# Low parts of the weights fetched in attention: made by GpSimd instead of VectorE

## The chip, the cores and the metric

The kernel runs on one core of a Trainium2 chip. Its metric is the device time of one execution in microseconds (us); lower is better. TensorE is called PE here, VectorE DVE, ScalarE ACT, GpSimd POOL and SyncE SP, as the profile's rows have them. SP only issues DMAs here.

## The reference, cut to what matters

One layer of a decoder, 1024 rows by 1024 columns, in float32:

```
h = rms_norm(x, attn_norm_w)
q, k, v, u, g = split(h @ w_in)            # 1024 x 7168 weights
# branch A: 8 heads, each with two score maps of 64 columns
p = softmax(q1 k1^T * scale + bias) - lam * softmax(q2 k2^T * scale + bias)
a = rms_norm(p @ v, subln_w) * (1 - lam_init);  y_a = a @ w_proj_attn
# branch B: causal convolution over 31 rows, for each channel
c = conv(u_a * sigmoid(u_b)) + conv_b
y_b = silu(layer_norm(c)) @ w_proj_conv
x = x + (sigmoid(g_a) * y_a + sigmoid(g_b) * y_b) @ w_out
h = rms_norm(x, ffn_norm_w)
x = x + (silu(h @ w_gate) * (h @ w_up)) @ w_down
```

## The kernel before, in words

**Products in three parts.** Each large product of float32 numbers is made of three fast ones. A number is split in a high part, rounded to a shorter format by ACT (`split_hi`, a copy, L120), and a low part, the rest (`value - high`, a subtraction). The product is high x high + high x low + low x high (`mm3`, L168 to L170). So every block of weights that is loaded (`wraw`, 128 x 1024 numbers, two buffers) needs a high part (`whi`) and a low part (`wlo`, three buffers each). `wsplit` makes both: first the high part on ACT, then the low part through `low`. The function `low` asks a switch, `low_by_pool`: if it is set, the subtraction is POOL's (L131), else DVE's (L125, inside `split_lo`, which serves all other splits, too).

**Order of the work.** The stages are: the opening and the first stage (0 to about 300 us in the profile: the products for u, some of v and the first head's q and k, with the first half of the convolution on DVE beside them), attention (about 300 to 815), the two projections with the layer norm of the convolution, the merge, and the channel mixer. The switch is set at the end of the opening and cleared after the first stage, so attention's low parts are DVE's.

**Attention** is a list of 64 steps: 8 heads (h) with 8 blocks of 128 rows (i). A step of block i has these parts. PE makes scores (`sc`, L1289 and L1290) from the parts of q (`qs`) and k (`ks`). DVE adds the bias (`tb`, one buffer, loaded by SP from `t_d` for each head) and finds the minimum (L1291: writes `E` and `mn`). ACT takes the exponential (L1296). DVE joins the two maps of a head (L1303, L1304, L1306: both inputs of L1306 are in SBUF). One step later PE turns `E` in blocks (`pT`, L1328), ACT makes the high part of the turned block (`ph`), DVE the low part (`pl`, from the turned block in PSUM). For each pair of blocks PE multiplies with v (`pW`), ACT copies the result (`ar`), PE turns it back (`pB`), and at a head's end comes the norm (`pS`, L1362). Of the two tiles `ph` and `pl` POOL sets a corner to zero for each pair (L1318, L1319); both have one buffer, so POOL waits there until PE has used the pair before.

Beside these 64 steps PE works through a list of products from h (`pg`, L168 to L170, where the weights come in): the next head's q and k, and g. The function `more` puts them between the steps. They need new weights: `ws` loads them (SP, into `wraw`) and splits them two blocks ahead of use (`ws.ahead = 2`). The products for q and k are scaled on DVE (L807), turned (`pQ`) and split again (L822, L824, `klo`), and shifted between halves of the partitions by DMAs (L826 to L837).

In the background DVE runs the second half of the convolution: channel tiles 4 to 7, 30 taps each (`bg`, L594, `acc` = `acc` + weight x `u`). The sums of tiles 0 to 3 (first stage) are in PSUM, those of tiles 4 to 7 in SBUF. A tile's sums are stored by SP (`c_d`), and POOL issues a DMA that adds them up over the tiles (L578, `cs_d`). POOL also issues the DMAs that make `t_d` (L776).

At the end of attention the finished heads are read back (`early`), split (`aTh`, `aTl`), and the first projection begins (`pg<-aTh,whi`).

**Who sets the order.** Each engine works through its own queue strictly in turn, and an instruction that waits holds all behind it. The queues are filled by a scheduler in the building step, which follows the program and its own idea of how long things take; so a change of one instruction's engine can move many others. The steps' shares of background taps are set by numbers in the kernel (`slack_of`), which don't change.

Of the kernel before, what the change touches and what calls it, by code (L numbers as in the profile page):

```python
# [57 lines left out]
def kernel(  # L58
# [68 lines left out]
    low_by_pool = [False]  # L127
# [1117 lines left out]
        due -= int(due)  # L1245
    while late:
        late.pop(0)[1]()
    low_by_pool[0] = False
    pcv_ctx.close()
    pgs.pop()  # L1250
    pg2_ctx.close()
# [264 lines left out]
    with after(m):  # L1516
        for _ in fill:
            pass
    inatt[0] = False
    del pms[1:]  # L1520
    at_ctx.close()

# [612 lines left out]
```

## Time and profile before

| what | us |
|---|---|
| median of 3 runs (1726.63 to 1727.03) | 1726.91 |
| span of the profiled execution | 1725.7 |
| median less that span: what lies around it | 1.2 |
| DVE busy in the span | 1275.4 |
| ACT busy in the span | 862.5 |
| DVE busy from 0 to 300 us | 228.14 |
| POOL busy from 0 to 300 us | 199.05 |

How to read it: a row of the profile names the source line (L125), the engine, the operation, the tiles as out<-in with buffer numbers left out, the shape, and the count; then busy us, mean ns of one, and the idle time of the engine just before with what ended it. A row of the timeline starts with the start and the length in us, and ends in brackets with the idle time before it, where there was any; `x3` means three merged. A row of the waits names who waited for whom, the sum in us, the number of times and the longest. PE's matmuls overlap, so their lengths are longer than the time from one start to the next.

### The profile page before, as it was taken

The numbers are of one execution on the slowest core, as the hardware profiler recorded it, in microseconds if no ns is written. First come the engines' busy times: TensorE is split into PE (matmuls) and PEld (weight loads), VectorE is DVE, ScalarE is ACT, GpSimd is POOL, SyncE is SP. The second block draws the span as 40 slices with busy tenths as digits, with TensorE's granted clock in tenths as the row PEclk, the third lists the DMA queues.
The fourth block names the chain that finished last, engine by engine and source line by source line (L and its number), as shares of the span: only waits on it lengthen the run. The fifth ranks groups of instructions, "written<-read, shape, count | busy, mean of one in ns | idle before, by whom it ended". The sixth has DMA issues, their size and how long they took to land.

```text
span 1725.7 us, 25863 instructions
## 1 busy us (share of the span) xinstructions
PE 1714.6 (99%) x9243; PEld 1477.9 (86%) x9243; DVE 1275.4 (74%) x2128; ACT 862.5 (50%) x1958; POOL 219.1 (13%) x207
## 2 busy tenths in 40 slices
PE   9999999999999999999999999999999999999999
PEld 7997889998998998988788888888888888888887
DVE  7675889898988888878687769966676666575544
ACT  5333335767777776756556325633333333333332
POOL 3997851000000000000000000000000000000000
PEclk9999999999999999999999999999999999999999
DMA  6344445336345344343973683245455445598663
GB/s 208 116 126 132 131 151 154 104 109 171 104 127 147 115 125 138 101 136 130 333 238 118 200 296 119 74 135 164 147 170 170 154 141 164 175 355 285 217 215 130
DMA packets 261604, 281.64 MB, mean 163 GB/s; under 512 B 16546, under 2 KB 181986, under 8 KB 261475
## 3 DMA queue, kind: packets, MB, share of 16 engines
q1 hardware_dynamic: 254160, 267.71, 48.3%
q0 software_dynamic: 5680, 9.39, 2.6%
q10 hardware_dynamic: 1634, 2.89, 0.5%
q8 instruction: 73, 1.20, 0.3%
q14 instruction: 57, 0.46, 0.1%
HBM read 181.84 MB, written 85.50 MB: 155 GB/s over the span
## 4 chain that ended last, share of the span: by engine, by line
PE 92%; DMA 3%; DVE 2%; ACT 1%; issue 1%; POOL 0%; SPq 0%; DVEq 0%; POOLq 0%; ACTq 0%
PE acc L980 29%; PE acc L488 12%; PE pg L168 12%; PE pg L169 12%; PE pg L170 12%; PE wo L1850 3%; PE sc L1290 2%; PE sc L1289 2%; PE pT L1328 2%; PE pg L1106 1%; DVE acc L594 1%; PE pW L168 1%; PE pW L169 1%; PE pW L170 1%; PE pQ L815 1%
## 5 line engine op out<-in xcount | busy, mean ns | idle before, releaser
L594 DVE SCALAR_TENSOR_TENSOR acc<-u,cw,acc 128x1023 f32<-128x1023 f32 (+14 forms) x240 | 303.4, 1264 | 23.2 <-ACT acc L588 20.7
L170 PE MATMUL pg<-whi,hT_lo 128*128 128x256 f32 x704 | 200.2, 285 | 0.0
L168 PE MATMUL pg<-whi,hT_hi 128*128 128x256 f32 x704 | 199.7, 285 | 0.4 <-DVE v L125 0.4
L169 PE MATMUL pg<-wlo,hT_hi 128*128 128x256 f32 x704 | 199.5, 284 | 0.0
L125 DVE TENSOR_TENSOR wlo<-draw,whi 128x1024 fp32r<-128x1024 f32 x75 | 91.7, 1223 | 83.4 <-ACT whi L120 78.9
L120 ACT CAST whi<-draw 128x1024 fp32r<-128x1024 f32 x75 | 79.1, 1055 | 129.5 <-PE acc L488 114.3
L169 PEld LDWEIGHTS pg<-wlo,hT_hi 128*128 128x128 f32 x704 | 134.4, 191 | 1.8
L170 PEld LDWEIGHTS pg<-whi,hT_lo 128*128 128x128 f32 x704 | 134.3, 191 | 1.8
L168 PEld LDWEIGHTS pg<-whi,hT_hi 128*128 128x128 f32 x704 | 134.0, 191 | 2.1 <-DVE v L125 0.6
L120 ACT CAST whi<-wraw 128x1024 fp32r<-128x1024 f32 x90 | 94.7, 1052 | 70.6 <-PE pg L169 32.6
L488 PE MATMUL acc<-wlo,whi 128*128 128x512 f32 x308 | 119.8, 389 | 0.0
L488 PE MATMUL acc<-whi,wlo 128*128 128x512 f32 x308 | 119.8, 389 | 0.0
L1296 ACT ACTIVATE E<-E,mn 128x640 f32<-128x640 f32 (+7 forms) x128 | 99.8, 781 | 30.8 <-DVE mn L1291 29.2
L168 PE MATMUL pg<-hT_hi,whi 128*128 128x512 f32 x288 | 114.4, 397 | 0.1
L169 PE MATMUL pg<-hT_lo,whi 128*128 128x512 f32 x288 | 113.7, 395 | 0.0
L170 PE MATMUL pg<-hT_hi,wlo 128*128 128x512 f32 x288 | 113.7, 395 | 0.0
L120 ACT CAST whi<-s 128x1024 fp32r<-128x1024 f32 x54 | 56.9, 1053 | 104.9 <-PE acc L980 101.8
L125 DVE TENSOR_TENSOR wlo<-wraw,whi 128x1024 fp32r<-128x1024 f32 x75 | 93.3, 1246 | 12.6 <-ACT whi L120 12.3
L1291 DVE CUSTOM_DVE_ANT_0 E<-sc,tb 128x512 f32<-128x512 f32 (+3 forms) x128 | 74.2, 585 | 33.2 <-PE pT L1328 16.1
L980 PE MATMUL acc<-h_hi,whi 128*128 128x512 f32 x240 | 93.4, 389 | 0.0
L980 PE MATMUL acc<-h_lo,whi 128*128 128x512 f32 x240 | 93.4, 389 | 0.0
L980 PE MATMUL acc<-h_hi,wlo 128*128 128x512 f32 x240 | 90.1, 389 | 0.0
(370 smaller groups left out, 4589.7 us busy)
## 6 DMA issues: line engine op xcount, KB each, us to landing
wraw<-in_w_gate_up_dram SPq DMA_DIRECT2D x44, 512.0 KB, 4.7
wraw<-in_w_in_dram SPq DMA_DIRECT2D x38, 512.0 KB, 4.0
qs<-qs SPq DMA_DIRECT2D x96, 128.0 KB, 2.3
wd<-in_w_down_dram SPq DMA_DIRECT2D x44, 256.0 KB, 3.1
tdT<-wd SPq DMA_DIRECT2D x88, 128.0 KB, 4.8
draw<-sdS SPq DMA_DIRECT2D x44, 256.0 KB, 3.7
draw<-tdT SPq DMA_DIRECT2D x44, 256.0 KB, 3.7
wraw<-in_w_in_dram SPq DMA_DIRECT2D x32, 256.0 KB, 3.3
```

Source lines behind the costliest of these rows:

```text
L120: act.copy(dst, src)
L125: last_lo[0] = dve.tensor_tensor(dst, src, f32(hi), op=ALU.subtract).ins
L168: pe.matmul(o, lh, rh, start=start, stop=False)
L169: pe.matmul(o, lh, rl, start=False, stop=False)
L170: last_mm[0] = pe.matmul(o, ll, rh, start=False, stop=stop).ins
L488: m = pe.matmul(o[s_][i][:], l_[:, ts], r_[:, 512:], start=start and j + y_ == 0, stop=j == n - 1 and y_ == 2, skip_group_check=not start,)
L594: dve.scalar_tensor_tensor(a_, us[c][:, : S - n], cw[:, c, t : t + 1], a_, op0=ALU.mult, op1=ALU.add)
L980: last_mm[0] = pe.matmul(o[:], a_[x_][:, k, :], b_[y_][:, k, :], start=start and k + x_ + y_ == 0, stop=k == 3 and x_ == 1, skip_group_che ...
L1289: pe.matmul(o[:, :w], qh[:, qs], k, start=True, stop=False)
L1291: dve.tensor_tensor_reduce(e[:, ks], o[:, :w], tb[:, S - nk + c0 : S - nk + c0 + w], 1.0, mn[:, j : j + 1] if c0 else 3.0e38, ALU.add, ALU ...
L1296: act.activation(e[:, :nk], e[:, :nk], AF.Exp, bias=mn[:, j : j + 1], scale=-1.0, accum_out=l[:, j : j + 1])
L1850: last_mm[0] = pe.matmul(o[s_][i][:], A[u_], B[v_], start=start and j + y_ == 0, stop=j == 3 and y_ == 2, skip_group_check=not start,).ins
```

## The change

The line that clears the switch moves from the end of the first stage to the end of attention:

```
--- before
+++ after
     while late:
         late.pop(0)[1]()
-    low_by_pool[0] = False
     pcv_ctx.close()
...
         for _ in fill:
             pass
     inatt[0] = False
+    low_by_pool[0] = False
     del pms[1:]
     at_ctx.close()
```

So the low parts of all weights that are fetched in attention, those for q, k and g and the first ones of the projection, are POOL's: 30 instructions of 128 x 1024. Their data, sizes and buffers stay. Lines after 1248 have numbers smaller by one in the changed kernel, up to the line that came in. The scheduler writes the queues anew from the start of attention; from the first projection on they are the same again.

Here is POOL's queue at the end of head 2 and the start of head 3, before. `pl` and `ph` are the memsets, the numbers are buffers.

```order
L1319 MEMSET pl_628_5090 128x128
L1318 MEMSET ph_627_5089 128x128
L1319 MEMSET pl_669_5359 128x128
L1318 MEMSET ph_668_5358 128x128
L1319 MEMSET pl_705_5547 128x128
L1318 MEMSET ph_704_5546 128x128
```

The same place of POOL's queue in the changed kernel:

```order
L1318 MEMSET pl_628_5090 128x128
L1317 MEMSET ph_627_5089 128x128
L1318 MEMSET pl_669_5359 128x128
L1317 MEMSET ph_668_5358 128x128
L131 TENSOR_TENSOR wlo_602_4877<-wraw_600_4873,whi_601_4876 128x1024
L131 TENSOR_TENSOR wlo_701_5515<-wraw_699_5511,whi_700_5514 128x1024
L131 TENSOR_TENSOR wlo_742_5686<-wraw_740_5683,whi_741_5685 128x1024
L1318 MEMSET pl_705_5547 128x128
```

Three low parts now stand between memsets of one pair and of the next; the first of them comes behind the memsets of buffers 669 and 668.

The end of attention in POOL's queue, before; `cs_d` is the DMA that adds the last channel tile's sums.

```order
L1319 MEMSET pl_1423_9593 128x128
L1318 MEMSET ph_1422_9592 128x128
L1319 MEMSET pl_1450_9707 128x128
L1318 MEMSET ph_1449_9706 128x128
L578 DMA cs_d_145<-c_d7_144 512x256
```

The same place in the changed kernel:

```order
L1318 MEMSET pl_1423_9593 128x128
L1317 MEMSET ph_1422_9592 128x128
L578 DMA cs_d_145<-c_d7_144 512x256
L131 TENSOR_TENSOR wlo_1457_9772<-wraw_1455_9769,whi_1456_9771 128x1024
L1318 MEMSET pl_1450_9707 128x128
L1317 MEMSET ph_1449_9706 128x128
```

The DMA and a low part now come ahead of the last pair's memsets.

PE's queue at this place, before, where the last pair of blocks of the last head is turned and multiplied:

```order
L1328 MATMUL pT_1451_9710<-ident_78,E_1427_9608 128x128
L1328 MATMUL pT_1454_9742<-ident_78,E_1444_9690 128x128 x2
L1348 MATMUL pB_1460_9803<-ident_78,ar_1441_9686 128x128 x2
L168 MATMUL pW_1462_9811<-ph_1449_9706,vh7_9162 128x256
L169 MATMUL pW_1462_9811<-pl_1450_9707,vh7_9162 128x256
```

The last rows of the same in the changed kernel:

```order
L168 MATMUL pg_1458_9775<-hT_hi_324,whi_1402_9469 128x512
L169 MATMUL pg_1458_9775<-hT_lo_325,whi_1402_9469 128x512
L170 MATMUL pg_1458_9775<-hT_hi_324,wlo_1403_9470 128x512
L1347 MATMUL pB_1460_9803<-ident_78,ar_1441_9686 128x128 x2
L168 MATMUL pW_1462_9811<-ph_1449_9706,vh7_9162 128x256
L169 MATMUL pW_1462_9811<-pl_1450_9707,vh7_9162 128x256
```

Between the pT of buffer 1454 and the pB there are now 19 matmuls of `pg` (the last three are shown), most of which stood further up before.

More of the change, by code (lines that the diff above doesn't have):

```diff
@@ L1247 @@
         late.pop(0)[1]()
-    low_by_pool[0] = False
     pcv_ctx.close()
@@ L1519 @@
     inatt[0] = False
+    low_by_pool[0] = False
     del pms[1:]
```

## The prediction

> **What bounds the kernel now.** I read the page first, then the waits and the busy time of the stretch that the change touches, the instruction groups of VectorE and GpSimd (DVE and POOL in the rows), and at last the timeline at single places.
>
> ```profile
> span 1725.7 us, 25863 instructions
> PE 1714.6 (99%) x9243; PEld 1477.9 (86%) x9243; DVE 1275.4 (74%) x2128; ACT 862.5 (50%) x1958; POOL 219.1 (13%) x207
> PE 92%; DMA 3%; DVE 2%; ACT 1%; issue 1%; POOL 0%; SPq 0%; DVEq 0%; POOLq 0%; ACTq 0%
> 300.00:815.00 515.00, 512.77 (x3435) 469.51 (x3434) 441.36 (x977) 363.14 (x1200) 18.11 (x71) 1.00 0.44 124
> PE sc L1289 <- DMA ks<-klo: 1.1, 1, 1.1
> PE sc L1290 <- DMA qs<-qs: 0.8, 1, 0.8
> PE pg L168 <- ACT sgg L639: 0.4, 1, 0.4
> PE pg L169 <- DVE aTl L125: 0.2, 1, 0.2
> ```
>
> The first three lines are the page: TensorE (PE) is busy 99% of the span and is 92% of the chain that ended last. The fourth is attention, from 300 to 815 us; its figures are PE, weight loads, DVE, ACT and POOL busy, then the granted clock (1.00) and the DMA share. PE stands idle for 515 - 512.77 = 2.23 us there, DVE for 515 - 441.36 = 73.64, and POOL is nearly free. The last four are all that PE waited for between 300 and 830 us: 2.5 us, and no row names a low part of a weight. So DVE's time is not what sets the end. The median of the runs, 1726.91, is the span and 1.2 us around it; I take my terms from the span and add them to 1726.91.
>
> **What is moved.** The order shows 30 low parts going from DVE to POOL, and nothing else leaves or comes; the other rows are the same work in another order. The groups between 300 and 815 us give the price on DVE, and the group of the stage before gives it on POOL, for the same shape.
>
> ```profile
> L125 DVE TENSOR_TENSOR wlo<-wraw,whi 128x1024 fp32r<-128x1024 f32 x30 | 36.6, 1219 | 2.8 <-ACT whi L120 2.7
> L131 POOL TENSOR_TENSOR wlo<-wraw,whi 128x1024 fp32r<-128x1024 f32 x15 | 36.2, 2414 | 49.6 <-ACT whi L120 49.6
> L594 DVE SCALAR_TENSOR_TENSOR acc<-u,cw,acc 128x995 f32<-128x995 f32 (+14 forms) x122 | 153.7, 1260 | 2.9 <-ACT acc L588 2.8
> L1306 DVE SCALAR_TENSOR_TENSOR E<-E,rl,E 128x640 f32<-128x640 f32 (+3 forms) x64 | 52.1, 814 | 0.6
> L807 DVE TENSOR_TENSOR qkraw<-qkraw,r 128x1024 f32<-128x1024 f32 x14 | 17.0, 1218 | 0.0
> ```
>
> DVE loses 30 x 1.219 = 36.6 us of work, POOL gains 30 x 2.414 = 72.4 us. POOL has 515 - 18.11 = 497 us free, so its own time hides.
>
> **Is a low part late?** It is needed when TensorE first loads it. The shortest lead that POOL's work of before, put in the new order, leaves inside attention is at the start of head 3. By buffer number this is the high part cast at 461.76, and its low part's first matmul is at 479.14.
>
> ```profile
> 461.76 1.07 ACT L120 CAST whi<-wraw 128x1024 fp32r<-128x1024 f32 x1
> 463.41 1.22 DVE L125 TENSOR_TENSOR wlo<-wraw,whi 128x1024 fp32r<-128x1024 f32 x1
> 468.65 0.21 POOL L1319 MEMSET pl<- 128x128 f32 x1 [21.20 <-PE pW L169]
> 468.81 0.21 POOL L1318 MEMSET ph<- 128x128 f32 x1
> 479.14 0.28 PE L169 MATMUL pg<-wlo,hT_hi 128*128 128x256 f32 x1
> ```
>
> On DVE it was done at 464.63, 14.5 us early. In the new order POOL reaches it only behind two memsets that wait for a pW matmul; they end at 469.0, so the low part ends at 469.0 + 2.4 = 471.4, still 7.7 us early. Behind it on POOL stands the next low part (done by 473.9) and nothing that others wait for sooner. The raw buffer it reads comes free 6.9 us later than before, and the SP queue holds the next raw load until then, with the ks copies of head 3 behind it.
>
> ```profile
> 468.26 0.72 SPq L836 DMA_DIRECT2D ks<-klo  x1
> 498.41 0.22 PE L1289 MATMUL sc<-ks,qs 128*128 128x128 f32 x1
> ```
>
> Those copies were issued at 468.26 and are first read at 498.41, so 30 us cover a delay of a few. Cost of lateness: 0, and if the cover went, PE would wait by the missing part.
>
> **What DVE and POOL do to each other.** In attention they have hardly been busy together, but before it there are places where they were.
>
> ```profile
> 49.02 4.78 DVE L272 TENSOR_TENSOR lprod<-lamt 128x64 f32<-128x64 f32 x2
> 56.94 2.57 DVE L125 TENSOR_TENSOR wlo<-wraw,whi 128x1024 fp32r<-128x1024 f32 x1
> 48.95 7.12 POOL L896 TENSOR_TENSOR F<-hT_hi,hT_lo 128x1024 f32<-128x1024 f32 x3
> 56.04 9.09 POOL L905 TENSOR_TENSOR F<-F,F 128x1024 f32<-128x1024 f32 x3
> 67.46 2.40 POOL L905 TENSOR_TENSOR F<-F,F 128x1024 f32<-128x1024 f32 x1
> 11.38 0.69 DVE L125 TENSOR_TENSOR hT_lo<-px,hT_hi 128x512 fp32r<-128x512 f32 x1 [0.74 <-ACT hT_hi L120]
> 10.95 2.38 POOL L1133 TENSOR_TENSOR vwl<-wraw,vwh 128x1024 fp32r<-128x1024 f32 x1 [9.63 <-ACT vwh L120]
> ```
>
> Two DVE products of 64 columns took 4.78 us, 2.39 each, just what one POOL instruction beside them took (7.12 / 3 = 2.37). A DVE low part took 2.57 instead of 1.22, and POOL's three took 9.09 where one alone takes 2.40. These DVE operations read two tensors from SBUF. The one at 11.38 reads one of its two from PSUM and kept its 0.69 beside a running POOL instruction. So one waits for the other's whole instruction if both of DVE's inputs lie in SBUF. [...]
>
> In attention the convolution taps (L594) have their sums in SBUF for the four channel tiles left, and L1306 and L807 read two SBUF tensors as well: 153.7 + 52.1 + 17.0 = 222.8 us of DVE's time. So a DVE operation will often meet a low part on POOL. One low part costs DVE between 0 (none meets it) and 2.41 us (one meets it at its start). I take the middle, 1.2, since a DVE operation of this kind is running or next about half the time (222.8 of 515). That is 30 x 1.2 = 36 us of waiting in place of 36.6 us of work: **DVE gains nothing**, 0.6 us. At the upper end it has 72.3 - 36.6 = 35.7 us more, still under its 73.64 us of idle time.
>
> **The end of attention.** PE has small gaps here that the list of waits leaves out.
>
> ```profile
> 808.53 0.68 DVE L125 TENSOR_TENSOR pl<-pT,ph 128x512 fp32r<-128x512 f32 x1
> 811.62 1.25 DVE L594 SCALAR_TENSOR_TENSOR acc<-u,cw,acc 128x994 f32<-128x994 f32 x1
> 814.62 0.49 PE L1328 MATMUL pT<-ident,E 128*128 128x128 f32 x3
> 815.24 0.44 PE L1348 MATMUL pB<-ident,ar 128*128 128x128 f32 x2
> 815.83 0.35 PE L168 MATMUL pW<-ph,vh 128*128 128x256 f32 x1
> 816.49 0.28 PE L168 MATMUL pW<-ph,vh 128*128 128x256 f32 x1
> 817.60 1.04 POOL L578 DMA_DIRECT2D cs_d<-c_d  x1 [2.46 <-DMA c_d<-acc]
> 826.88 0.40 PE L170 MATMUL pg<-aTh,wlo 128*128 128x512 f32 x1
> 439.39 0.33 PE pT L1328 x3
> 376.62 0.24 PE pB L1348 x2
> ```
>
> The last two rows are of the chain: three transposes back to back take 0.33 from start to start and two take 0.24. So pB could have begun at 814.95 and the next pW at 815.19: 815.83 - 815.19 = 0.64 us lost, some 0.9 with the matmuls right behind. In the new order 19 matmuls of pg lie between pT and pB, which cover this: -0.9. Against it, POOL's queue now has L578 and a low part ahead of the last two memsets, for which the second group of three pW matmuls (816.49) waits. L578 waits for the store of the sums, and that for the last tap. This tap ran at 811.62; now it stands just ahead of the split that ran at 808.53, so it ends some 4 us sooner. L578 then comes near 814, the low part ends near 814 + 1.0 + 2.4 = 817.4, and the memsets near 817.8: 0 to 1.3 us after 816.49. I take +0.9, because PE itself reaches that matmul later by what was put in front.
>
> **Sum:** 0 (low parts in time) - 0 (DVE) - 0.9 + 0.9 = 0, so 1726.9.
>
> **Rivals.** *A, the freed DVE pays.* If few POOL low parts meet a DVE operation, DVE runs up to 36.6 us shorter, and the waits that PE has (2.23 in the stretch, 0.6 behind it, 0.9 at the end) all go: -3.7, 1723.2. For it: the wait of 1.1 us for ks is for a copy of klo, which DVE makes. Against it: the qs wait of 0.8 is for a chain of copies, and there is nothing beyond 3.7 to win.
>
> [...] Where a low part holds DVE for 2.41 us instead of the 1.22 that it worked there, results reach PE 1.19 us later. Mostly they have room, but not everywhere.
>
> ```profile
> 564.75 0.75 DVE L1306 SCALAR_TENSOR_TENSOR E<-E,rl,E 128x512 f32<-128x512 f32 x1
> 565.70 0.49 PE L1328 MATMUL pT<-ident,E 128*128 128x128 f32 x3
> ```
>
> Here pT began 0.2 us after DVE had made its E. It decides from the point where DVE's lead over PE is under 1.19 us when a low part runs. If that is so at a third of the 30, with half of 1.19 lost at each, it is 10 x 0.6 = +6, 1733; all 30 in full would be +35.7, which the 73.64 us of idle DVE time exclude as a likely case. [...]
>
> *C, POOL's queue.* A low part stuck behind memsets or L578 arrives after its matmul. The smallest lead left is 7.7 us inside attention, and at the end the low part done near 817.4 is first read at 826.88, so it would need a wait on POOL several us longer than any here; 2 to 4 us, 1730.
>
> That the change does nothing is no rival: the 30 rows stand under POOL in the order.
>
> **Numbers.** A difference of 0.2% (3.45 us) is about what a measurement of this kernel can tell from none. My forecast, no change, 0.55; A 0.2; B 0.2; C 0.05. A lies just past the bound, so faster is 0.2, B and C make slower 0.25. The range takes in A with 1 us to spare, and B: 1722.0 to 1733.0.
>
> **What would show it.** Right: 30 low parts under POOL L131 with a mean of 2.4 to 3 us between 300 and 815; the mean of L594 there up from 1.26 to about 1.5, with DVE's busy time within some 10 us of 441; PE idle 1 to 4 us there. A would show L594 at 1.26, DVE near 405 and no wait of PE. B would show PE waiting for L1306, L125 or scores, 5 us or more in all. C would show PE waiting for POOL L131. I am wrong if PE waits long for anything in this stretch, or if the time leaves 1723.5 to 1730.3.

## The result, and the profile after

The changed kernel takes 1741.28 us (median of 4 runs, 1739.87 to 1742.28), the kernel before 1726.77 beside it: a ratio of 1.0083, 95% interval 1.0071 to 1.0095. It is 14.5 us slower, past the prediction's range.

The page of the changed kernel, its first lines and the chain:

```profile
span 1740.5 us, 25873 instructions
PE 1719.2 (99%) x9243; PEld 1479.1 (85%) x9243; DVE 1288.7 (74%) x2098; ACT 860.4 (49%) x1958; POOL 296.1 (17%) x237
PE 81%; DVE 9%; DMA 4%; ACT 3%; issue 2%; SPq 0%; POOL 0%; DVEq 0%; ACTq 0%
```

DVE gave 30 x 1.219 = 36.6 us of work away and is busy 1288.7 - 1275.4 = 13.3 us longer. So the instructions it kept take 49.9 us more. In the chain DVE rose from 2% to 9%. Here is the same stretch of attention as in the prediction (PE, weight loads, DVE, ACT, POOL busy), and below it what PE waited for from 290 to 850 us, the six longest:

```profile
300.00:815.00 515.00, 505.17 (x3382) 459.93 (x3381) 451.42 (x938) 357.19 (x1190) 92.36 (x98) 1.00 0.43 122
```

```profile
PE sc L1288 <- DVE mn L1290: 2.3, 5, 1.1
PE pS L1368 <- DVE an L1361: 1.5, 2, 0.9
PE pT L1327 <- DVE qs L824: 1.2, 1, 1.2
PE pQ L815 <- DVE qkraw L807: 1.2, 1, 1.2
PE pB L1347 <- ACT ar L1341: 1.1, 1, 1.1
PE pT L1327 <- DVE E L1305: 1.0, 1, 1.0
```

PE's idle time in the stretch is 9.83 us where it was 2.23. It waits for results of DVE in many places, none of them long, and never for a low part on POOL (L131). The groups of DVE and POOL in this stretch say why DVE is late:

```profile
L594 DVE SCALAR_TENSOR_TENSOR acc<-u,cw,acc 128x995 f32<-128x995 f32 (+14 forms) x121 | 162.3, 1342 | 8.7 <-ACT acc L588 8.5
L131 POOL TENSOR_TENSOR wlo<-wraw,whi 128x1024 fp32r<-128x1024 f32 x29 | 75.3, 2601 | 190.9 <-ACT whi L120 184.8 <-PE sc L1289 2.8 <-DMA ks<-klo 2.1
L1305 DVE SCALAR_TENSOR_TENSOR E<-E,rl,E 128x640 f32<-128x640 f32 (+7 forms) x63 | 58.1, 923 | 0.8
L807 DVE TENSOR_TENSOR qkraw<-qkraw,r 128x1024 f32<-128x1024 f32 x14 | 19.2, 1370 | 0.2
L657 DVE TENSOR_TENSOR r<-r,t 128x16 f32<-128x16 f32 (+1 forms) x21 | 11.1, 530 | 0.3
L682 DVE TENSOR_SCALAR v<-ssa 128x8 f32<-128x8 f32 x7 | 6.8, 968 | 2.1 <-ACT jk L1356 2.1
```

The taps rose from 1260 to 1342 ns, L1305 (L1306 before) from 814 to 923. The surprise is in the last two, tiny steps of a norm, which the prediction did not look at. Before, they read:

```profile
L657 DVE TENSOR_TENSOR r<-r,t 128x16 f32<-128x16 f32 (+1 forms) x21 | 3.5, 168 | 0.1
L682 DVE TENSOR_SCALAR v<-ssa 128x8 f32<-128x8 f32 x7 | 1.1, 164 | 0.0
```

One place in the timeline of the changed kernel shows how it comes about; the first two rows are DVE, then POOL, then PE:

```profile
327.15 2.37 DVE L657 TENSOR_TENSOR r<-r,t 128x16 f32<-128x16 f32 x1
329.44 3.21 DVE L1305 SCALAR_TENSOR_TENSOR E<-E,rl,E 128x768 f32<-128x768 f32 x1
326.61 5.23 POOL L131 TENSOR_TENSOR wlo<-wraw,whi 128x1024 fp32r<-128x1024 f32 x2 [13.95 <-ACT whi L120]
331.29 0.39 PE L168 MATMUL pg<-hT_hi,whi 128*128 128x512 f32 x1
332.71 0.87 PE L1327 MATMUL pT<-ident,E 128*128 128x128 f32 x6 [1.04 <-DVE E L1305]
```

Two low parts run back to back on POOL. L657, 0.17 us of work, is stopped behind the first one for 2.2 us; L1305, 1.0 us of work, behind the second for another 2.2. PE then has nothing left but pT, which needs this E. Taking each DVE instruction beside a POOL subtraction between 295 and 850 us, its length less that of the same line and shape elsewhere, gives 46.3 us for the 30 low parts, 1.54 each. I call this sum the stops below; another choice of what is set beside what moves such a sum by some 1 us. Over half of it, some 25 us, falls on the short steps of the norm and the softmax (L655 to L657, L682, L1303), and only some 10 us on the taps.

### The profile page after: what moved, and what is told of

It is laid out like the page before. It is cut to its first block, busy times and chain, and to the rows that moved or that the text cites. A ratio compares the mean times of both kernels' runs of the same rounds, so it can differ in the third digit from the quotient of the medians.

```text
span 1740.5 us, 25873 instructions
## 1 busy us (share of the span) xinstructions
PE 1719.2 (99%) x9243; PEld 1479.1 (85%) x9243; DVE 1288.7 (74%) x2098; ACT 860.4 (49%) x1958; POOL 296.1 (17%) x237
## 4 chain that ended last, share of the span: by engine, by line
PE 81%; DVE 9%; DMA 4%; ACT 3%; issue 2%; SPq 0%; POOL 0%; DVEq 0%; ACTq 0%
PE acc L980 30%; PE acc L488 12%; PE pg L168 9%; PE pg L169 9%; PE pg L170 9%; PE wo L1850 3%; DVE acc L594 2%; DVE E L1290 1%; PE sc L1289 1%; DVE E L1305 1%; PE sc L1288 1%; PE pg L1106 1%; PE pT L1327 1%; ACT E L1295 1%; PE pW L170 1%
## 5 line engine op out<-in xcount | busy, mean ns | idle before, releaser
L594 DVE SCALAR_TENSOR_TENSOR acc<-u,cw,acc 128x1023 f32<-128x1023 f32 (+14 forms) x240 | 313.3, 1305 | 28.6 <-ACT acc L588 26.0
L131 POOL TENSOR_TENSOR wlo<-wraw,whi 128x1024 fp32r<-128x1024 f32 x45 | 114.1, 2541 | 239.7 <-ACT whi L120 213.4
L980 PE MATMUL acc<-h_hi,wlo 128*128 128x512 f32 x240 | 90.1, 389 | 0.0
L1290 DVE CUSTOM_DVE_ANT_0 E<-sc,tb 128x512 f32<-128x512 f32 (+3 forms) x128 | 73.9, 583 | 19.1 <-PE pT L1327 6.5
```

Source lines behind the costliest of these rows:

```text
L131: pool.tensor_tensor(dst, src, f32(hi), op=ALU.subtract)
L594: dve.scalar_tensor_tensor(a_, us[c][:, : S - n], cw[:, c, t : t + 1], a_, op0=ALU.mult, op1=ALU.add)
L980: last_mm[0] = pe.matmul(o[:], a_[x_][:, k, :], b_[y_][:, k, :], start=start and k + x_ + y_ == 0, stop=k == 3 and x_ == 1, skip_group_che ...
L1290: dve.tensor_tensor_reduce(e[:, ks], o[:, :w], tb[:, S - nk + c0 : S - nk + c0 + w], 1.0, mn[:, j : j + 1] if c0 else 3.0e38, ALU.add, ALU ...
```

## The experiments

Theory L: POOL's subtraction and DVE's operations stop each other; DVE's results come late, and PE waits. Rival O: the new order of the queues costs the time, whatever POOL does. Rival Q: low parts or raw buffers come late behind POOL's queue. The short diffs show only the lines that matter; in them, `att[0]` is a switch that is set where the kernel before cleared `low_by_pool` and cleared at the end of attention.

The building step may write the queues anew for each run. To see how far, I lined up DVE's instructions in two traces by operation, tiles and shape (285 to 870 us, without the low parts). Between the kernel before and the changed kernel 67% stand in the same order; between the changed kernel and run 1 it is 88%. The changed kernel and run 4, runs 5 and 6, and runs 8 and 11 agree in more than 99%. Runs 2, 3, 7 and 8 agree in 71 to 79% with the run that they are set beside, so there a difference of a few us can come from the order.

**1. Memsets in place of the subtractions.**

```
-        if low_by_pool[0]:
+        if att[0]:
+            pool.memset(f32(dst), 0.0)
+        elif low_by_pool[0]:
             pool.tensor_tensor(dst, src, f32(hi), op=ALU.subtract)
```

> The changed kernel, but in attention GpSimd fills the low part with zeros instead of subtracting (the subtraction is left out, so the low parts of attention's weights count as zero). [...] Theory O (the new order of the queues costs the time, whatever GpSimd does): still 1738 to 1743. Theory Q (low parts or raw buffers come late behind GpSimd's queue): 1726 to 1735, with PE waiting for L131's place in the queue no less than before.

Measured: 1726.39 us against 1726.70, ratio 0.9998 (0.9989 to 1.0007). Attention in this run, and its memsets:

```profile
300.00:815.00 515.00, 514.68 (x3453) 472.30 (x3452) 413.22 (x949) 361.89 (x1202) 47.22 (x102) 1.00 0.46 129
```

```profile
L132 POOL MEMSET wlo<- 128x1024 f32 x30 | 29.5, 984 | 203.2 <-PE pg L173 144.7 <-PE pg L172 57.1 <-DVE mn L1294 1.4
```

The order is near that of the changed kernel, the place of the work is the same, and PE is idle for 0.32 us. L gives 1724 to 1729 here, with DVE busy for the 441.36 - 36.6 = 405 us that are left to it; it is busy 413 us, 8 more. O falls as the main cause: it is what POOL does that costs. With memsets of 984 ns in their place PE waits 0.3 us for a minimum of DVE, where it was 2.3; and the 62 short memsets of the kernel before in this stretch, 0.2 us each, lengthened the DVE instructions beside them by 0.4 us in all.

**2. Each subtraction twice.**

```
             pool.tensor_tensor(dst, src, f32(hi), op=ALU.subtract)
+            if att[0]:
+                pool.tensor_tensor(dst, src, f32(hi), op=ALU.subtract)
```

> The changed kernel, with each of attention's 30 subtractions done twice in a row on GpSimd. Theory L: VectorE loses some 46 us more (its busy time in attention from 456 to about 500 us, near its limit), so PE loses at least another 14 us: 1755 to 1775. Theory O: 1741, as only the order counts and it is nearly the same. Theory Q: each low part is 2.4 us later, which the leads of 7.7 us and more cover: 1741 to 1745, and what is added shows as waits for L131 or for the raw loads.

Measured: 1782.64 us, ratio 1.0327 (1.0313 to 1.0341). The stops are 90.1 us, twice those of the changed kernel, as L has it; but the time is above L's range. The waits of PE up to 900 us, the three longest:

```profile
PE pS L1372 <- DVE an L1365: 13.9, 5, 4.5
PE sc L1292 <- DVE mn L1294: 7.6, 5, 3.4
PE pT L1331 <- DVE E L1309: 6.2, 4, 2.8
```

All are for DVE, and no row of the list names L131 or a raw load: Q falls. 44 us of stops more go with 41 us of time more. The granted clock was 0.97 in attention here and 1.00 in the changed kernel; how much of the 41 us that makes is not shown. The single steps are longer, too (`an`, L1365, took 2.21 us on the mean of six, 1.53 in the changed kernel and 1.22 before), so the sum isn't the only thing that grew.

**3. A subtraction on POOL that nobody needs, the low parts on VectorE.**

```
+        if att[0]:
+            split_lo(dst, src, hi)
+            pool.tensor_tensor(src, src, f32(hi), op=ALU.subtract)
-        if low_by_pool[0]:
+        elif low_by_pool[0]:
```

> VectorE makes attention's low parts as in the kernel before, and GpSimd then does one more subtraction of the same size for each, into the raw buffer, whose result nobody uses. Theory L: VectorE busy 441 + some 46 = 487 us in attention, without the 36.6 us that the change takes from it, so worse than the changed kernel: 1745 to 1765. Theory O: the work moved nowhere: 1727, or a few us either way as the queues are written anew. Theory Q: raw buffers come free 2.4 us later: 1727 to 1731.

Measured: 1744.13 us, ratio 1.0103 (1.0089 to 1.0117), with stops of 42.1 us. It moves no work and costs 17.4 us, so the stops make a slower kernel without any move; O allowed a few us for its own order of the queues. L's range began at 1745, 0.9 us too high.

**4. The copy of ar ahead of the splits.** This came from the end of attention, where the changed kernel loses time that no DVE row explains. First two rows of ACT, then some rows of PE:

```profile
830.60 2.03 ACT L120 CAST aTh<-early 128x1024 fp32r<-128x1024 f32 x2 [7.54 <-DMA early<-a_d]
833.96 0.38 ACT L1341 COPY ar<-pW 128x256 f32<-128x256 f32 x1
832.88 0.39 PE L170 MATMUL pg<-hT_hi,wlo 128*128 128x512 f32 x1
834.39 0.44 PE L1347 MATMUL pB<-ident,ar 128*128 128x128 f32 x2 [1.12 <-ACT ar L1341]
835.34 0.49 PE L168 MATMUL pg<-aTh,whi 128*128 128x512 f32 x1 [0.51 <-ACT aTh L120]
836.60 0.50 PE L169 MATMUL pg<-aTl,whi 128*128 128x512 f32 x1 [0.77 <-DVE aTl L125]
838.32 0.63 PE L170 MATMUL pg<-aTh,wlo 128*128 128x512 f32 x1
840.79 0.40 PE L170 MATMUL pg<-aTh,wlo 128*128 128x512 f32 x1
```

ACT waits 7.54 us for two heads that are read back (`early`), and behind the wait in its queue stand the norm's steps and `ar`. Before, the same copy came first:

```profile
817.04 0.37 ACT L1342 COPY ar<-pW 128x256 f32<-128x256 f32 x1
817.31 1.05 ACT L120 CAST aTh<-early 128x1024 fp32r<-128x1024 f32 x1
```

The edit puts the old order of these back:

```
-    for h in range(2, 5):
-        early_split(h)
+    with after(last_of(mybir.EngineType.Activation)):
+        for h in range(2, 5):
+            early_split(h)
```

> The changed kernel, but at the end of attention ScalarE's queue has the copy of the last pW block (ar, L1341) ahead of the splits of the heads read back (aTh), as in the kernel before; the rest of the order is the changed kernel's. Theory L with a tail: in the changed kernel ScalarE waits 7.5 us there for two reads (early) while pB needs ar, and PE has 2.2 us more of gaps behind 815 us than before; undone, 1738.5 to 1740. Theory L alone: the reads end as late in either case and the tail costs nothing of its own: 1741 to 1742.

Measured: 1735.48 us, ratio 1.0052 (1.0039 to 1.0064). That is 5.8 us less than the changed kernel and below the expected range, which ended at 1738.5. From 832.88 to 840.79 PE begins 12 matmuls of 512 columns, 0.23 us each when nothing waits, and two of 128, 0.11 each: 3.0 us of work in 7.9, so 4.9 us lost. In a part of this the granted clock was lower: from 838.32 to 840.46 five matmuls of 512 columns begin 0.43 us apart, with no wait between them. The busy times and the granted clock (the third number from the end) in the changed kernel:

```profile
832.00:837.00 5.00, 2.60 (x11) 1.48 (x10) 3.73 (x4) 4.80 (x12) 0.00 (x0) 1.00 0.57 162
837.00:841.00 4.00, 4.00 (x11) 2.75 (x10) 3.21 (x4) 3.76 (x10) 0.00 (x0) 0.57 0.19 70
```

In the first 5 us PE was busy 2.60 at a clock of 1.00; in the 4 us behind them the clock was 0.57. In run 4 it was 1.00 from 815 to 860 us. So the 14.5 us fall into two: some 5.8 for the order of ACT's queue at the end (the one place where O is right), and 8.8 for the stops.

**5. Memsets, with the copy first.** The edits of 1 and 4 together.

> The run with memsets for the low parts (subtraction left out), with ScalarE's queue at the end of attention as in the run with the copy first. PE had 3.9 us of gaps behind 815 us in the run with memsets, 2.5 of them at the pB that waits for ar. If the price of that order of ScalarE's queue adds to the port's, as the two runs before suggest, this gives 1723 to 1724.5, and says what VectorE's relief is worth without a lock: 2.5 to 4 us less than the kernel before. If the tail's price hangs on the lock, 1726 as without.

Measured: 1722.22 us, ratio 0.9974 (0.9963 to 0.9984), 0.8 below the expected range and 4.2 us below run 1. So the order of ACT's queue has its price without stops, too, if not the same one (4.2 here, 5.8 beside the subtractions, where the clock was 0.57 for 4 us as well). The run also tells what the relief of DVE, a clean end of attention and the new order of the queues are worth together without stops: 4.2 us, and no more. So the 8.8 us above are net: run 4 lies 13.3 above this one, and this one 4.2 to 4.5 below the kernel before.

**6. A GpSimd operation with one input.**

```
+        if att[0]:
+            pool.tensor_copy(dst, f32(hi))
+        elif low_by_pool[0]:
```

> The changed kernel with the copy first, but GpSimd copies the high part into the low part's tile instead of subtracting (the subtraction is left out): an operation of the same size that reads one tensor instead of two. [...]

Measured: 1721.87 us, ratio 0.9973 (0.9962 to 0.9983). I had expected 1728 to 1736 if a POOL instruction with one input is enough to stop DVE as before, and 1722 to 1726 if it takes two inputs. The time fits the second case, but the trace shows stops as in the first: the copies do stop DVE, 11 times for over half a us, at most 0.84, and for 9.2 us in all. They are short, 1.33 us on the mean. Here is a step of 0.16 us that one of them stops, then all copies:

```profile
647.11 1.01 DVE L685 TENSOR_SCALAR v<-ssa 128x8 f32<-128x8 f32 x1
646.30 1.79 POOL L132 CAST wlo<-whi 128x1024 fp32r<-128x1024 f32 x1 [15.30 <-ACT whi L120]
L132 POOL CAST wlo<-whi 128x1024 fp32r<-128x1024 f32 x30 | 39.8, 1325 | 221.8 <-ACT whi L120 195.1 <-DVE rl L1306 12.0 <-PE pS L1372 11.4
```

So this copy with one input from SBUF was enough to stop DVE. In run 5, with memsets in its place and nearly the same order of DVE's queue, DVE was busy 413.76 us in attention, here 420.65. The 9 us of short stops cost nothing that can be measured (1721.87 against 1722.22).

**7. Four pieces.**

```
+        if att[0]:
+            for c in range(0, 1024, 256):
+                q = slice(c, c + 256)
+                pool.tensor_tensor(dst[:, q], src[:, q], f32(hi)[:, q], op=ALU.subtract)
+        elif low_by_pool[0]:
```

Run 4 with each subtraction on POOL in 4 pieces of 256 columns.

> [...] If it is the single long stop (up to 2.2 us, more than the lead of a result that PE waits for) that costs, stops of at most some 0.7 us give 1724 to 1730. If it is the sum of the stops (46 us of VectorE's time, which pieces don't shorten, as VectorE stops at each piece anew), 1735 as without pieces, or worse, as four pieces take longer than one.

Measured: 1730.37 us, ratio 1.0019 (1.0009 to 1.0028): 5.1 us less than the whole subtractions of run 4, just above the range of the first case.

```profile
L134 POOL TENSOR_TENSOR wlo<-wraw,whi 128x256 fp32r<-128x256 f32 x117 | 107.5, 949 | 198.7 <-ACT whi L120 153.8 <-DVE E L1311 19.7 <-PE pB L1353 13.3
```

A low part now takes 4 x 0.949 = 3.8 us on POOL, longer than whole (2.6). The stops fell to 26.3 us, which the expectation had not foreseen: both the sum and the single stop became smaller, so this run doesn't tell the two apart. For each us of stops it costs no less than run 4: 8.2 us above run 5 for 26.3, where run 4 is 13.3 above it for 46.0. Of PE's waits here, 2.9 us are for copies of q (qs, 0.5 in run 4).

**8. Every second low part.**

```
+        if att[0]:
+            turn_[0] += 1
-        if low_by_pool[0]:
+        if low_by_pool[0] and not (att[0] and turn_[0] % 2):
```

> The changed kernel, but only every second low part of attention is GpSimd's, the others VectorE's as before. The end of attention has ScalarE's queue in the order of the kernel before here. If each low part has its own price, half of the 8.7 us that the run with the copy first still lost: 1729 to 1733. If the price comes only when VectorE as a whole runs out of time, less than a quarter of it: 1725 to 1729.

Measured: 1724.75 us, ratio 0.9991 (0.9982 to 1.0000), with stops of 20.9 us. It is just below the second range, but that case's reason isn't borne out: VectorE as a whole doesn't run out of time in run 4, where it is busy 453 of 515 us, against 447 here. Half of the low parts cost far less than half: against the 1722.2 of run 5 it is +2.5, where all 30 (run 4) are +13.3.

**9 and 10. Without the taps in attention.** The copy first as in run 4; the low parts on POOL (9) or on DVE (10).

```
-                dve.scalar_tensor_tensor(a_, us[c][:, : S - n], cw[:, c, t : t + 1], a_, op0=ALU.mult, op1=ALU.add)
+                if not att[0]:
+                    dve.scalar_tensor_tensor(a_, us[c][:, : S - n], cw[:, c, t : t + 1], a_, op0=ALU.mult, op1=ALU.add)
```

> The changed kernel with the copy first, without the convolution taps that VectorE runs in attention (about 120 of 1.25 us left out, so the convolution's sums of the last four channel tiles lack them). VectorE then idles some 150 us more in attention. Beside it stands the same with the low parts on VectorE. If the price came from VectorE's queue as a whole (results late behind the taps and behind the stops that taps make), it is gone: this run within 1 us of its twin. If it comes from the single stops of the short steps between PE and VectorE (L657, L682, L1303, L1305 were stopped for up to 2.2 us each), half or more of the 8.7 us stay: 4 us or more above its twin.

> The twin of the run without taps: the low parts of attention on VectorE as in the kernel before, everything else as there (taps in attention left out, the copy first at the end). With 150 us less on VectorE, PE should wait for it nowhere: 1720 to 1724.

Measured: 1733.78 us (ratio 1.0041, 1.0028 to 1.0053) with POOL, 1731.58 (1.0029, 1.0017 to 1.0040) with DVE. Run 10 is far above what I expected. The longest waits of PE in run 9, then in run 10:

```profile
PE sc L1291 <- DMA ks<-klo: 5.8, 1, 5.8
PE pQ L817 <- DVE qkraw L809: 1.2, 1, 1.2
PE pT L1330 <- DVE E L1308: 1.0, 1, 1.0
```

```profile
PE sc L1291 <- DMA qs<-qs: 3.9, 1, 3.9
PE sc L1292 <- DMA qs<-qs: 1.7, 1, 1.7
```

Without the taps the queues are written in another way, and both runs lose some 5.7 us at one place, to copies of q and k that come late; I did not follow why. Beside that the twins differ by 2.2 us, between the two cases, and their intervals overlap. In run 9 the two long single waits of the changed kernel remain (qkraw 1.2, E 1.0), and the many small ones for the minimum, the norm and qs are gone but for 0.6. But leaving the taps out also took away stops: run 9 has some 20 us of them, not 46, and run 8 with 20.9 cost 2.5. So these runs don't show how the 8.8 us divide between a queue of DVE that runs late as a whole and single stops between PE and DVE.

**11. Every second low part, in four pieces.** Runs 7 and 8 together pointed to it.

```
+        if att[0]:
+            turn_[0] += 1
-        if low_by_pool[0]:
-            pool.tensor_tensor(dst, src, f32(hi), op=ALU.subtract)
+        if low_by_pool[0] and not (att[0] and turn_[0] % 2):
+            step = 256 if att[0] else dst.shape[-1]
+            for c in range(0, dst.shape[-1], step):
+                q = slice(c, c + step)
+                pool.tensor_tensor(dst[:, q], src[:, q], f32(hi)[:, q], op=ALU.subtract)
```

> Every second low part of attention on GpSimd, each in 4 pieces of 256 columns. Four pieces took VectorE 26 us instead of 46 for 30 low parts, so some 11 to 13 us here instead of the 20.9 of every second part whole, with VectorE's busy time near 438 us instead of 447. If the remaining waits of PE (1.3 us for a minimum on VectorE) hang on that, 1723 to 1724.5, below the 1724.75 of every second part whole; if pieces only change the order by chance, 1724 to 1728.

Measured: 1722.97 us against 1726.77, ratio 0.9976 (0.9967 to 0.9985). It is at the lower edge of what was expected, 3.8 us below the kernel before and 18.3 below the changed one. Its stops are 13.8 us. Run 8 has nearly the same order of the queues of DVE and PE, so this pair shows what pieces bring by themselves: 1.8 us, and run 8's wait of 1.3 us for a minimum (`mn`) is gone. Attention and the 45 us behind it:

```profile
300.00:815.00 515.00, 515.00 (x3456) 472.23 (x3455) 441.64 (x965) 365.00 (x1209) 76.50 (x133) 1.00 0.45 128
815.00:860.00 45.00, 44.55 (x201) 36.22 (x200) 28.99 (x43) 23.22 (x41) 0.00 (x0) 1.00 0.97 328
```

The second stretch in the kernel before:

```profile
815.00:860.00 45.00, 43.70 (x196) 34.99 (x196) 25.12 (x37) 23.44 (x45) 1.39 (x3) 1.00 0.97 332
```

PE is not idle at all in attention (2.23 us before), and 0.45 us behind it (1.30 before). DVE is as busy as before, 441.64 us, since the stops eat most of what it gave away (15 x 1.219 = 18.3 us). So it is not shown that the relief of DVE brings these 3 us; the order of the queues that came with it can have done it.

## Why the prediction was wrong, point by point

**Low parts in time: right.** PE waits for no L131, in the changed kernel and with everything doubled. POOL's 72 us do hide. (By its own rows the raw buffer comes free 6.8 us later, not 6.9; nothing hangs on it.)

**DVE waits beside POOL: right in kind, too small in size.** I took 1.2 us a low part, 36 in all; it is 1.54 and 46.3. The step was "a DVE operation of this kind is running or next about half the time (222.8 of 515)". It counted three lines by their busy time. But a stopped operation need not be long. L657, L682 and L1304 (L1303 in the changed kernel) have little busy time and are stopped as fully, for up to 2.2 us. The trace of before had such a row, which I passed over:

```profile
271.60 1.95 DVE L657 TENSOR_TENSOR r<-r,t 128x16 f32<-128x16 f32 x1
271.12 4.77 POOL L131 TENSOR_TENSOR wlo<-wraw,whi 128x1024 fp32r<-128x1024 f32 x2 [17.17 <-ACT whi L120]
```

L682 reads one tensor only and took 2.37 us at 657.64 instead of 0.16, so my "if both of DVE's inputs lie in SBUF" was too narrow. What the expectation of run 5 calls the port's price and the lock is these stops: no run shows a port, only that DVE's instructions beside POOL's subtractions were longer, by 46.3 us here.

```profile
657.64 2.37 DVE L682 TENSOR_SCALAR v<-ssa 128x8 f32<-128x8 f32 x1
656.84 3.14 POOL L131 TENSOR_TENSOR wlo<-wraw,whi 128x1024 fp32r<-128x1024 f32 x1 [15.30 <-ACT whi L120]
```

**"So DVE's time is not what sets the end", and 35.7 us "still under its 73.64 us of idle time": this step failed.** The stops' price was set against DVE's idle time as if that could be used at any moment. But DVE's order is fixed, and its idle time lies where it waits for PE and ACT (in the changed kernel's attention 13.3 us for PE at L1290, 10.8 for ACT at L1302, the two largest). When a stop of 2.2 us comes, the next results are late, and PE has only its own lead to bridge it, as at 329 us above. Net, the stops took no more of DVE than 46.3 - 36.6 = 9.7 us, far less than the idle time, and the kernel still lost 8.8 us beside the end of attention. Run 3 shows the stops without any moved work: +17.4 us with DVE still idle for 47 of 515 us. Against run 5, 20.9 us of stops cost 2.5 us (run 8), 26.3 in pieces 8.2 (run 7) and 46.0 13.3 (run 4). So the price isn't in proportion to the sum; what sets it beyond the sum is not shown, as the order of the queues differs among these.

**The end of attention, -0.9 + 0.9 = 0: this step failed, too.** It followed PE's and POOL's queues and not ACT's. There the splits of two heads that are read back had moved ahead of `ar`, and the wait for their reads, 7.54 us, held what PE needed. Undone by itself (run 4) this is 5.8 us, and 4.2 where memsets stand for the subtractions (run 5 against run 1). The memsets that I had priced at +0.9 cost nothing: the last low part ended at 824.1, and no wait for it shows.

**The rivals.** B was right in kind: waits of DVE beside POOL (46.3 us) in place of the work that left (36.6). Its price, +6, is 8.8 without the end of attention, and its chance, 0.2, was too small, because the idle time seemed to exclude the dear case. A was near on its size: the ceiling I put at 3.7 us is 4.2 in run 5 and 4.6 in run 6, where the order of the queues is new as well. C does not happen.

## What to carry to other kernels

Before work moves from VectorE to GpSimd, count what else VectorE does there, the tiny steps too, and allow for stops of VectorE beside GpSimd's subtractions and copies: here they were 1.54 us on the mean for a subtraction of 2.41 us, 0.31 for a copy of 1.33. Half as many cost a fifth here (run 8 against run 4), and with nearly the same order of the queues pieces saved another 1.8 us (run 11 against run 8). VectorE's idle time was no cover for the stops; what covers is the lead of each result over the engine that needs it. Where a scheduler writes the queues anew, look at every engine's queue at the places where something waits for a DMA, above all for a short copy that has fallen behind such a wait.

## What the runs showed of the hardware that I had not expected

Operations of 8 or 16 columns were stopped as fully as one of 1024 (2.37 us for L682 and for L657 instead of some 0.16; 3.40 for an L1361 of 1024 columns, at 474.38, instead of 1.22). Two kinds were never stopped beside a subtraction: L1302, a reciprocal with one input (7 cases, 0.05 us in all), and L1290, which reads its scores from PSUM (22 cases, under 0.1 us in all).

On POOL's side the copies that read one tensor, 1.33 us on the mean, stopped DVE for up to 0.84 us (run 6). Beside memsets of the same size, 0.98 us, DVE was busy 6.9 us less in attention (run 5).

In the changed kernel the granted clock was 1.00 from 832 to 837 us, where PE was busy for 2.60 of 5 us, and 0.57 in the 4 us behind, where matmuls of 512 columns begin up to 0.43 us apart with no wait between them, instead of 0.23. In run 1 the same place had this:

```profile
816.00:821.00 5.00, 3.15 (x13) 1.96 (x12) 3.84 (x4) 5.00 (x12) 0.00 (x0) 1.00 0.44 157
821.00:825.00 4.00, 3.84 (x17) 2.82 (x17) 3.26 (x4) 3.73 (x11) 0.00 (x0) 1.00 0.19 69
```

With 3.15 us busy of 5 the clock was 1.00 in both stretches. What sets it is not shown. The three waits of PE at this place in the changed kernel are 2.4 us in all (1.12, 0.51 and 0.77), and 4.9 us were lost there.
